# Ten pairs of a mixer's input projection by seven block products, the strided groups through scratch

## The chip, the cores and the metric

One core of a Trainium2 chip runs the whole kernel. The metric is the device time of one execution in microseconds; the time before is 2790.25 us, the median of three runs (2789.18 to 2790.53).

## The reference, cut to what matters

Two layers (`DEPTH = 2`) over 1024 tokens of 1024 features, all in float32. Each layer is a mixer and a gated feed-forward network:

```python
h = rmsnorm(x, norm1[l])
proj = h @ w_in[l]                       # 1024 x 5120
qa, ka, va, qb, kb, vb, gate_pre = jnp.split(proj, splits, axis=-1)
o_a = dilated_mixture(...qa, ka, va)     # 12 heads of 64: three groups of four, dilation 1, 4 and 16
o_b = stick_breaking_attention(...qb, kb, vb)   # 4 heads of 64
gates = jax.nn.sigmoid(gate_pre + b_gate[l])
merged = g_a * (o_a @ w_br[l, :OUT_A]) + g_b * (o_b @ w_br[l, OUT_A:])
x = x + merged @ w_o[l]
h2 = rmsnorm(x, norm2[l]); up = h2 @ w_up[l]     # conv, gelu, product, w_down
```

The 5120 columns of `w_in` are 40 chunks of 128: for mixer A six chunks each of q, k and v (two for each of its three groups), for mixer B two each of q, k and v, and 16 gate chunks. `dilated_mixture` weighs the three groups of a head slot by their softmax denominators.

## The kernel before

**Precision.** Each float32 operand of a large product is split into a rounded part and its remainder (`split`: a cast on ScalarE, L115, and a subtraction on VectorE, L116). A product of two split operands is three matmuls (hi x hi, lo x hi, hi x lo; `product`, L141 to L143). The normed input lies in `H[n]`, n being the half of the tokens (512 each), features on the partitions in eight blocks. One chunk of 128 output columns is 2 halves x 8 blocks x 3 = 48 matmuls of 128x512.

**Feed-forward network.** 20 of its 22 up-projections (`up`, a gate chunk and a value chunk together) are already worked out by seven block products in place of eight. The operands are cut in two by two blocks; sums of weight blocks are formed per pair on GpSimd and VectorE (L1139, L1140, L1144, L1149), sums of the input's blocks (`S[1]` to `S[4]`) once a layer; `seven` issues one block product of 4 x 3 = 12 matmuls, and three additions on VectorE put the seven results together. The down-projection is done so too.

**Mixer.** `head` works out v, k and q of mixer B's first pair of heads (four chunks). Then `attend` walks over 36 items: 16 stick-breaking ones (B), 4 near ones of group 0 (N), 16 far ones (T) that take the groups of dilation 4 and 16 together for one head slot and one residue r. An item is a list of small steps: scores, then alternately the turning of probabilities (transposes into bank `t`, split into p1h and p1l) and the application to the values (bank `o`). Between the steps `attend` calls `dense.advance(rate)`, which takes steps of six projection matmuls from a `Dense` object. Its `main` list holds the chunks that attention waits for (names like `b1`, `00`, `v1`), each with the items that must be done first; its `fill` list holds the 16 gate chunks, which nobody waits for. `RATE` gives the dense steps per attention step for the B, N and the two halves of the T items. The next item's scores are worked out among the steps of the item before, if its operands are there. TensorE's order is exactly the order of this walk (a manual schedule); the other engines' and SyncE's DMA queue's orders are set by a scheduler from the same program.

**Strided groups.** Groups 1 and 2 keep k and q in SBUF, each with its remainder, in an order by residue (`view`, `grid`: tokens r, r+4, ... next to each other); their values come out with features on the partitions and are transposed (`values_tiled`, bank v_t, L426) into an SBUF tile each. Everything stays in SBUF from projection to use.

**End of attention.** After the last far item of a pair of head slots, `join` (L743 on) reads the near group's statistics from scratch (sn), forms the weights by small operations (L755 to L764), writes them to scratch (df, L765), reads them back spread over partitions (fn, ft, L770), scales and adds (L771, L775, L776). `dense.finish()` then issues what is left of the dense work; then `on` and `ob` are split into the operands oh_a, ol_a, oh_b, ol_b, and 32 branch products (bank br_ps, weights br_w) follow, gated by gates read back from scratch (gin), then w_o.

Of the kernel before, what the change touches and what calls it, by code (L numbers as in the profile page):

```python
# [15 lines left out]
P = 128  # L16
# [16 lines left out]
PT = 5  # L33
# [7 lines left out]
RATE = (0.68, 0.85, 1.0, 0.8)  # L41
# [8 lines left out]
def trunk_kernel(ctx, tc, x, norm1, w_in, b_gate, w_br, w_o, norm2, w_up, conv_w, conv_b, w_down, norm_f, out, depth=None, probe=None):  # L50
# [50 lines left out]
    gd = dr.tile([NF // 2, 7, P, 2, HF], F32, name="gd")  # L101
    dn = [dr.tile([4, T], F32, name=f"dn{i}") for i in range(2)]
# [8 lines left out]
    def big(name, dtype=F32):  # L111
        return sb.tile([P, 2, T], dtype, tag="e8", bufs=6, name=name)

# [67 lines left out]
    class Dense:  # L181

        def __init__(self):
            self.main, self.fill, self.done = [], [], set()
            self.now = self.nxt = None
            self.due = 0.0

        def choose(self):  # L190
            if self.main and self.main[0][1] <= self.done:
                name, _, gen = self.main.pop(0)
            elif self.fill:
                name, gen = None, self.fill.pop(0)
            else:
                return None
            next(gen)
            return name, gen

        def step(self):  # L200
            while True:
                if self.now is None:
                    self.now = self.nxt or self.choose()
                    if self.now is None:
                        return False
                    self.nxt = self.choose()
                if next(self.now[1], 0) != 0:
                    return True
                self.done.add(self.now[0])
                self.now = None  # L210

        def advance(self, rate):
            self.due += rate
            while self.due >= 1.0:
                self.due -= 1.0
                if not self.step():
                    self.due = 0.0

        def until(self, names):
            while not set(names) <= self.done:  # L220
                assert self.step(), (names, self.done)

        def finish(self):
            while self.step():
                pass

# [77 lines left out]
    def new_x(n):  # L304
        X[n] = sb.tile([P, KD, HF], F32, tag=f"x{n}", name=f"x{n}")
# [4 lines left out]
    def norm_add(n, e, first=False, sub=slice(0, HF), adds=None):  # L310
# [6 lines left out]
        act.activation(sq, X[n][:, e, sub], AF.Square)  # L317
# [3 lines left out]
    def gain_in(n, e, sub=slice(0, HF)):  # L321

        x = X[n][:, e, sub]
# [36 lines left out]
    def norm(n, gain, tag, then=None, keep=False):  # L360
# [17 lines left out]
        for e in range(KD):  # L378
            hf = kept_f32(n, e) if keep else small("hf")
            dve.scalar_tensor_tensor(hf, X[n][:, e, :], gain[:, e : e + 1], rb, ALU.mult, ALU.mult)  # L380
# [9 lines left out]
    def values(key, l, off, tag):  # L390
        w = weights(w_in[l][:, off : off + 256], 256)
        yield
        vt = R[key] = sb.tile([P, 8, 4, P], F32R, tag=tag, name="v_" + tag)
        yield from values_part(vt, w, range(4))

    def values_part(vt, w, ms):
        for m in ms:
# [13 lines left out]
            vv = vt[:, 2 * m : 2 * m + 2, :, :]  # L411
# [4 lines left out]
    def values_tiled(key, l, off, tag):  # L416


        w = weights(w_in[l][:, off : off + 256], 256)
        yield  # L420
        vt = R[key] = sb.tile([P, 8, 4, P], F32R, tag=tag, name="v_" + tag)

        def turn(c, n, f):
            tp = bank("ps", "v_t")
            for r in range(4):
                pe.transpose(tp[:, r * P : (r + 1) * P], f[:, r * P : (r + 1) * P], ident)  # L426
            tv = tp.rearrange("p (r h c) -> p r h c", r=4, h=2)
            vv = vt[:, 4 * n : 4 * n + 4, 2 * c : 2 * c + 2, :]
            act.copy(vv[:, :, :, 0:64], tv)
            dve.tensor_tensor(vv[:, :, :, 64:128], tv, f32(vv[:, :, :, 0:64]), ALU.subtract)  # L430

        last = None
        for n in range(2):
            for c in range(2):
                o = bank("ps", "v_ps")
                yield from product(o, [((wh[:, c * P : (c + 1) * P], wl[:, c * P : (c + 1) * P]), h_part(n, k)) for k, (wh, wl) in enumerate(w)])
                f = small("vf")
                act.copy(f.rearrange("p (r j) -> p r j", r=4), grid(o, True))
                if last:
                    turn(*last)  # L440
                last = (c, n, f)
                yield
        yield
        turn(*last)
        yield


    def view(t, tiled, n):

        if tiled:  # L450
            return t.rearrange("p (r n j) -> p n r j", r=4, n=2)[:, n, :, :]
        return t[:, n * HF : (n + 1) * HF]

    def grid(o, tiled):
        return o.rearrange("p (j r) -> p r j", r=4) if tiled else o

    def keys_half(kt, w, n, tiled):
        o = bank("ps", "k_ps")
        yield from product(o, [(w[k], h_part(n, k)) for k in range(KD)])
        og = grid(o, tiled)  # L460
        ka, kb = view(kt[:, 0, :], tiled, n), view(kt[:, 1, :], tiled, n)
        act.copy(ka[0:64], og[0:64])
        act.copy(kb[64:128], og[64:128])
        dve.tensor_tensor(ka[64:128], og[0:64], f32(ka[0:64]), ALU.subtract)
        dve.tensor_tensor(kb[0:64], og[64:128], f32(kb[64:128]), ALU.subtract)
        yield

    def queries_half(q, w, n, tiled, scale):
# [3 lines left out]
        og = grid(o, tiled)  # L472
        qa, qb, la, lb = (view(a[:, i, :], tiled, n) for a in (qt, ql) for i in range(2))
        for q2, src in ((qa, og[0:64]), (qb, og[64:128])):
            act.mul(q2[0:64], src, scale)
            act.mul(q2[64:128], src, scale)
        dve.scalar_tensor_tensor(la[0:64], og[0:64], scale, f32(qa[0:64]), ALU.mult, ALU.subtract)
        dve.scalar_tensor_tensor(lb[64:128], og[64:128], scale, f32(qb[64:128]), ALU.mult, ALU.subtract)
# [10 lines left out]
    def keys(key, l, off, tiled):  # L489
# [3 lines left out]
        for n in range(2):  # L493
            yield from keys_half(kt, w, n, tiled)

    def queries(key, l, off, tiled, scale):
# [3 lines left out]
        for n in range(2):  # L500
            yield from queries_half(q, w, n, tiled, scale)

    def head(l):
# [9 lines left out]
        vt = R["vb"] = sb.tile([P, 8, 4, P], F32R, tag="x0", name="vb")  # L513
# [3 lines left out]
        for n in range(2):  # L517
            yield from keys_half(kt, wk, n, False)
            yield from queries_half(q, wq, n, False, SCALE)
# [3 lines left out]
    def scores(o, s, q, k, qs, ks):  # L523
        qt, ql = q
        pe.matmul(o, qt[:, s, qs], k[:, s, ks], start=True, stop=False, skip_group_check=True)
        pe.matmul(o, ql[:, s, qs], k[:, s, ks], start=False, stop=True, skip_group_check=True)  # L526
# [17 lines left out]
    def stick_item(pr, s, qp):  # L544
# [6 lines left out]
        def score(a):  # L551
# [6 lines left out]
            for c0 in range(0, L, 512):  # L558
                w = min(512, L - c0)
                z = bank("s", "z")  # L560
                scores(z[:, :w], s, q, k, slice(i * P, i * P + P), slice(c0, c0 + w))
# [20 lines left out]
        def apply(kb):  # L582
# [4 lines left out]
            for j in range(2):  # L587
                c = P if last and j else 0
                for p in (0, 1):
                    pe.matmul(  # L590
                        o[:, c:256],
                        vt[:, kb + j, hd, :],
# [5 lines left out]
            if last:  # L598
                fold(ob[64 * s : 64 * s + 64, pr, qp * 256 : (qp + 1) * 256], o)

# [4 lines left out]
    def near_item(pr, s):  # L605
        if s == 0:
            R["st0", pr] = sb.tile([P, 2, 2, 8], F32, tag="st0", bufs=2, name="st0")
        if "on" not in R:
            R["on"] = big("on")
# [4 lines left out]
        def score(m):  # L614
# [7 lines left out]
            for j in range(2):  # L622
# [3 lines left out]
                scores(zz, s, q, k, slice(b * P, b * P + P), slice((b - 1) * P + c, b * P + P))  # L626
# [17 lines left out]
        def apply(i, some, n, first, last):  # L644
# [4 lines left out]
            for kb, bs in some:  # L649
                c0, nb = (bs[0] - 4 * n) * P, len(bs) * P  # L650
                for p in (0, 1):
                    pe.matmul(
                        o[:, c0 : c0 + nb],
                        vt[:, kb, slot, :],
# [36 lines left out]
    def far_item(pr, s, r, share):  # L691
        slot = 2 * pr + s
        qk = [(R["q1", pr], R["k1", pr]), (R["q2", pr], R["k2", pr])]
# [834 lines left out]
```

## Time and profile before

| | |
|---|---|
| median of three runs | 2790.25 us |
| profiled execution: time, span | 2795.43 us, 2793.3 us |
| mean granted TensorE clock | 0.995 |
| TensorE busy, matmuls | 2723.8 us (98%), 13306 |
| VectorE, ScalarE, GpSimd busy | 67%, 47%, 19% |
| DMA | 355.5 MB, mean 127 GB/s |

The profile is of one execution. An engine's busy time is the sum of the stretches in which it had work; a group's mean is the duration of one instruction, and consecutive matmuls overlap, so their means add up to more than the busy time. The mixer of layer 0 takes about the first 650 us, that of layer 1 about 1400 to 2050 us. In the page's 40 slices TensorE is at nine tenths or more everywhere but the first, GpSimd is at zero or one tenth in the mixers, and the DMA engines are at one to three tenths there, with four to eight around the merges.

### The profile page before, as it was taken

Reading aid. Unit: us, or ns where it says so; the run is one execution under the profiler, and the core shown is the slowest. Engines: PE = TensorE matmul, PEld = TensorE weight load, DVE = VectorE, ACT = ScalarE, POOL = GpSimd, SP = SyncE. Lnnn points to the kernel's source line nnn. Section 1 sums busy time; section 2 is a strip of 40 time slices with the busy share of each in tenths; the row PEclk is TensorE's granted clock in tenths of the full one; section 3 lists DMA queues with packets and bytes.
Section 4 is the critical chain, followed back from the end, with each engine's and each line's share of the span. In section 5 each row is a group of like instructions: output and inputs, shape, how many; then the busy total and the mean of one; then the engine's idle time right before and its main releaser. Section 6 shows DMA issues by size and latency. Waiting matters only on the chain. (4 is left out here: it accounts for less than half of the span.)

```text
span 2793.3 us, 36113 instructions
## 1 busy us (share of the span) xinstructions
PE 2723.8 (98%) x13306; PEld 2278.0 (82%) x13306; DVE 1875.2 (67%) x2796; ACT 1326.2 (47%) x2410; POOL 518.1 (19%) x376
## 2 busy tenths in 40 slices
PE   8999999999999999999999999999999999999999
PEld 8878888888877778778888788888788787777888
DVE  5875434455778888897657754344658788888865
ACT  5655544454445545432345654335545455554225
POOL 0000000012134333331110000000212343443200
PEclk9999999999999999999999999999999999999999
DMA  3011113164334443688411111122822434436863
GB/s 122 24 46 54 36 53 80 61 212 132 87 113 160 142 151 129 217 317 300 154 50 35 42 43 46 58 72 71 262 88 78 151 130 149 164 138 240 336 230 121
DMA packets 285884, 355.52 MB, mean 127 GB/s; under 512 B 21532, under 2 KB 222604, under 8 KB 285196
## 3 DMA queue, kind: packets, MB, share of 16 engines
q1 hardware_dynamic: 285708, 353.22, 37.6%
q8 instruction: 105, 1.72, 0.2%
q14 instruction: 71, 0.58, 0.1%
HBM read 247.13 MB, written 106.04 MB: 126 GB/s over the span
## 5 line engine op out<-in xcount | busy, mean ns | idle before, releaser
L116 DVE TENSOR_TENSOR w_lo<-w_raw,w_hi 128x512 fp32r<-128x512 f32 x232 | 163.7, 709 | 147.6 <-ACT w_hi L115 139.0
L116 DVE TENSOR_TENSOR w_lo<-up_a,w_hi 128x512 fp32r<-128x512 f32 x240 | 231.7, 966 | 38.0 <-ACT w_hi L115 37.9
L115 ACT CAST w_hi<-w_raw 128x512 fp32r<-128x512 f32 x232 | 143.8, 621 | 201.0 <-PE o_ps L142 67.2
L115 ACT CAST w_hi<-up_a 128x512 fp32r<-128x512 f32 x240 | 149.4, 622 | 173.6 <-PE u_b L1124 38.5
L141 PE MATMUL g_ps<-hh,w_hi 128*128 128x512 f32 x512 | 211.6, 413 | 1.1 <-DVE v_x L430 1.1
L1284 DVE TENSOR_TENSOR x<-x,d_ps 128x512 f32<-128x512 f32 (+1 forms) x228 | 152.3, 671 | 82.7 <-PE d_ps L1278 81.8
L143 PE MATMUL g_ps<-hh,w_lo 128*128 128x512 f32 x512 | 201.1, 393 | 0.0
L142 PE MATMUL g_ps<-hl,w_hi 128*128 128x512 f32 x512 | 200.7, 392 | 0.0
L1003 POOL TENSOR_TENSOR cv<-cv 128x512 f32<-128x512 f32 x88 | 126.0, 1444 | 266.2 <-DVE g L116 130.1
L485 POOL MEMSET ql<- 64x1024 f32 x16 | 15.3, 955 | 831.4 <-PE z L526 643.2
L116 DVE TENSOR_TENSOR g<-cv,g 128x512 fp32r<-128x512 f32 x154 | 168.2, 1102 | 0.1
L1123 PE MATMUL u_a<-hh,w_hi 128*128 128x512 f32 x320 | 127.3, 398 | 19.4 <-ACT g L115 15.6
L1276 PE MATMUL d_ps<-gd_in,w_hi 128*128 128x512 f32 (+1 forms) x340 | 131.1, 385 | 5.8 <-ACT g L115 5.8
L1277 PE MATMUL d_ps<-gd_in,w_hi 128*128 128x512 f32 (+1 forms) x340 | 131.2, 386 | 0.0
L1278 PE MATMUL d_ps<-gd_in,w_lo 128*128 128x512 f32 (+1 forms) x340 | 131.0, 385 | 0.0
L1125 PE MATMUL u_a<-hh,w_lo 128*128 128x512 f32 x320 | 126.0, 394 | 4.1 <-DVE w_lo L116 4.1
L115 ACT CAST g<-cv 128x512 fp32r<-128x512 f32 x154 | 93.4, 620 | 75.4 <-DVE g L116 43.6
L1124 PE MATMUL u_a<-hl,w_hi 128*128 128x512 f32 x320 | 125.8, 393 | 0.0
L1123 PE MATMUL u_a<-t_hi,w_hi 128*128 128x512 f32 x320 | 124.6, 389 | 0.4 <-ACT u L1157 0.4
L1125 PE MATMUL u_a<-t_hi,w_lo 128*128 128x512 f32 x320 | 124.5, 389 | 0.0
L1124 PE MATMUL u_a<-t_lo,w_hi 128*128 128x512 f32 x320 | 124.5, 389 | 0.0
L143 PEld LDWEIGHTS g_ps<-hh,w_lo 128*128 128x128 f32 x512 | 96.1, 188 | 22.0
(335 smaller groups left out, 8056.5 us busy)
## 6 DMA issues: line engine op xcount, KB each, us to landing
gd<-g SPq DMA_DIRECT2D x154, 512.0 KB, 3.1
gd_in<-gd SPq DMA_DIRECT2D x154, 512.0 KB, 6.0
w_raw<-in_w_in_dram SPq DMA_DIRECT2D x160, 256.0 KB, 3.0
up_a<-in_w_up_dram SPq DMA_DIRECT2D x80, 512.0 KB, 4.5
wd_raw<-in_w_down_dram SPq DMA_DIRECT2D x22, 1024.0 KB, 9.1
gs<-gt SPq DMA_DIRECT2D x64, 256.0 KB, 2.1
gin<-gs SPq DMA_DIRECT2D x32, 512.0 KB, 4.4
w_raw<-in_w_o_dram SPq DMA_DIRECT2D x64, 256.0 KB, 2.8
```

Of the source, the lines that this page charges most:

```text
L115: act.copy(hi, src)
L116: dve.tensor_tensor(lo, src, f32(hi), ALU.subtract)
L141: pe.matmul(o, lh, rh, start=(first and i == 0), stop=False, skip_group_check=share)
L142: pe.matmul(o, lh, rl, start=False, stop=False, skip_group_check=share)
L143: pe.matmul(o, ll, rh, start=False, stop=(last and i == n - 1), skip_group_check=share)
L1123: pe.matmul(o, w[0][:, c], rh, start=(first and i == 0), stop=False, skip_group_check=True)
L1124: pe.matmul(o, w[0][:, c], rl, start=False, stop=False, skip_group_check=True)
L1125: pe.matmul(o, w[1][:, c], rh, start=False, stop=(last and i == 3), skip_group_check=True)
L1276: pe.matmul(o[:, sub], wh[:, c], gh[:, sub], start=(i == 0 and k in (0, 4, 5)), stop=False, skip_group_check=True)
L1277: pe.matmul(o[:, sub], wh[:, c], gl[:, sub], start=False, stop=False, skip_group_check=True)
L1278: pe.matmul(o[:, sub], wl[:, c], gh[:, sub], start=False, stop=(i == m - 1), skip_group_check=True)
L1284: dve.tensor_tensor(x, x, o[:, sub], ALU.add)
```

## The change

Of the 36 chunks that `attend` handles in a layer, 16 stay as they are: k and q of mixer B's second pair, values, k and q of group 0, and eight gate chunks (`PLAIN = 8`). The other 20 are worked out as ten pairs (`pair`): values, k and q of groups 1 and 2 (six pairs) and eight gate chunks (four pairs). A pair has seven block products of 12 matmuls, like `up`.

- `Dense` gets the lists `plain`, `seven` and `side`. The plain chunks come first; pairs start when the near items' scores are done (`N11s`) and no plain chunk is left. Six steps of a pair (`READY`) are prepared ahead: two loads, sums of weight blocks, splits.
- `block_sums` forms the sums `S[1]` to `S[4]` of the input's blocks a layer from H's parts, during the near items: 24 operations on GpSimd, 16 on VectorE and 16 splits.
- k and q of a strided group are written to scratch (`tk`), with q's remainder above a block of zeros that is filled once at the start (`none`); values go to `tv`. Each far item reads its own block (`fetch_kq`, 128x1536, and `fetch_v`, 128x512), two items' k and q and four items' values ahead; an item waits until `LEAD = 6` dense steps after its k and q were asked for.
- SBUF: x, the values, `on`, the fetched blocks and the sum share one tag `xa` of four tiles of 8 KB a partition. `ob` waits in scratch (`obd`) and is read back before the merge; x is moved in halves. `PT` is 6 for 5, the second half's rate 0.85 for 0.8.
- The gates' bias is added in the sigmoid, in two operations of 128x512 each, no longer when the gate is copied out.
- Two hooks, the split of `ob` and `on` and the first loads of the merge, are called from the last pair if attention is over by then, and otherwise after the dense work.

```diff
-PT = 5
+PT = 6
-RATE = (0.68, 0.85, 1.0, 0.8)
+RATE = (0.68, 0.85, 1.0, 0.85)
+PLAIN = 8
+LEAD = 6
...
+    def pair(dense, l, offs, tiled, put):
...
+        raw = sb.tile([P, 4, 512], F32, tag="ql", bufs=2, name="in_a")
+        for c in range(2):
+            nc.sync.dma_start(...w_in[l][:, offs[c] : offs[c] + P]...)
+        a11, a12, a21, a22 = (raw[:, i, :] for i in range(4))
+        yield
+        u = sb.tile([P, T], F32, tag="wr", bufs=NRAW, name="u")
+        u1, u2 = u[:, HF:T], u[:, 0:HF]
+        pool.tensor_tensor(u2, a11, a21, ALU.subtract)
+        pool.tensor_tensor(a21, a21, a22, ALU.add)
...
+        pa, pc = bank("ps", "i_a"), bank("ps", "i_c")
+        yield from seven(pa, w1, half(1, 0), True, True)
+        act.copy(view(u1), grid(pa))
+        w7 = piece(u2)
+        yield
+        yield from seven(pc, w5, S[1], True, True)
+        act.copy(view(u5), grid(pc))
+        w2 = piece(a12)
+        yield
+        yield from seven(pa, w6, S[2], False, True)
+        act.copy(view(u2), grid(pa))
+        w4 = piece(a22)
+        dense.last(0)
...
+        yield from seven(pc, w3, half(0, 1), False, True)
+        dve.tensor_tensor(view(u2), view(u2), grid(pc), ALU.add)
+        put(0, 0, u2, False)
...
+        yield from seven(pa, w7, S[3], False, True)
+        dve.tensor_tensor(view(u5), view(u5), grid(pa), ALU.add)
+        put(1, 0, u5, False)
+        dense.last(1)
...
+        pb = bank("ps", "i_b")
+        yield from seven(pb, w2, half(1, 1), True, True)
+        dve.tensor_tensor(view(u1), view(u1), grid(pb), ALU.add)
+        put(0, 1, u1, False)
...
+        for word in seven(pa, w4, S[4], False, True):
+            yield "turn"
+            yield
+        put(1, 1, grid(pa), True)
...
+    def fetch_kq(i):
+        t = R["kq", i] = sb.tile([P, 6, 256], F32R, tag="xa", bufs=4, name="t_kq")
+        nc.sync.dma_start(f32(t), tk[i // 8][i // 4 % 2, i % 4])
...
         dense.main = [
-            *kq("b", 1, set(), P, False, SCALE),
-            ("v0", set(), values("v0", l, OFF_VA, "x1")),
-            *kq("0", 0, {"B07s"}, 0, False, -SCALE),
-            *kq("0", 1, {"B17s"}, P, False, -SCALE),
-            ("v1", {"B17"}, values_tiled("v1", l, OFF_VA + 256, "x0")),
-            *kq("1", 0, {"N01s"}, 256, True, -SCALE),
-            *kq("2", 0, {"N11s"}, 512, True, -SCALE),
-            ("v2", {"N11"}, values_tiled("v2", l, OFF_VA + 512, "x1")),
-            *kq("1", 1, {"T07s"}, 256 + P, True, -SCALE),
-            *kq("2", 1, {"T07s"}, 512 + P, True, -SCALE),
+            *kq("b", 1, set(), P, SCALE),
+            ("v0", set(), values("v0", l, OFF_VA), False),
+            *kq("0", 0, {"B07s"}, 0, -SCALE),
+            *kq("0", 1, {"B17s"}, P, -SCALE),
+            (None, {"N11s"}, pair_v(dense, l, 1), True),
+            *((None, {"N11s"}, pair_kq(dense, l, g, 0), True) for g in (1, 2)),
+            (None, {"N11s"}, pair_v(dense, l, 2), True),
+            *((None, {"N11s"}, pair_kq(dense, l, g, 1), True) for g in (1, 2)),
         ]
...
         attend(dense, items)
-        dense.finish()
...
+        branches()
...
+        dense.hooks = [in_two, begin]
+        dense.finish()
+        for n in range(2):
+            new_x(n)
```

More of the change, by code (lines that the diff above doesn't have):

```diff
@@ L414, in values_part @@
             yield
[L416 to L445, printed above, removed]
@@ new lines, in pair_v, with turn, put @@
+    def pair_v(dense, l, g):
+        def turn(c, n, f):
+            tp = bank("s", "v_t")
+            for r in range(4):
+                pe.transpose(tp[:, r * P : (r + 1) * P], f[:, r * P : (r + 1) * P], ident)
+            tw = tp.rearrange("p (r h c) -> p r h c", r=4, h=2)
+            vv = sb.tile([P, 4, 2, P], F32R, tag="p4", bufs=4, name="vv")
+            act.copy(vv[:, :, :, 0:64], tw)
+            dve.tensor_tensor(vv[:, :, :, 64:128], tw, f32(vv[:, :, :, 0:64]), ALU.subtract)
+            for h in range(2):
+                there = tv[c][h, :, :, g - 1, n * P : (n + 1) * P]
+                nc.sync.dma_start(there.rearrange("r p c -> p r c"), f32(vv[:, :, h, :]))
+            if (c, n) == (1, 1):
+                dense.done.add(f"v{g}")
+        def put(c, n, x, psum):
+            f = x
+            if psum:
+                f = small("vf")
+                act.copy(f.rearrange("p (r j) -> p r j", r=4), x)
+            dense.at(2, lambda: turn(c, n, f))
+        off = OFF_VA + 256 * g
+        return pair(dense, l, (off, off + P), True, put)
@@ L779, in gate, with pair_gate, put @@
+    def pair_gate(dense, l, e):
+        def put(c, n, x, psum):
+            t = x
+            if psum:
+                t = small("gt")
+                act.copy(t, x)
+            nc.sync.dma_start(gs[e, n, :, c, :], t)
+        return pair(dense, l, (OFF_G + e * P, OFF_G + D + e * P), False, put)
     def gate(l, c):
```

383 lines of the change are left out of this document (272 added, 111 removed).

## The prediction

> **What bounds the kernel now.** I read the page first, its shares and TensorE's groups:
>
> ```profile
> span 2793.3 us, 36113 instructions
> PE 2723.8 (98%) x13306; PEld 2278.0 (82%) x13306; DVE 1875.2 (67%) x2796; ACT 1326.2 (47%) x2410; POOL 518.1 (19%) x376
> L143 PE MATMUL g_ps<-hh,w_lo 128*128 128x512 f32 x512 | 201.1, 393 | 0.0
> ```
>
> TensorE is busy 98% of the span and no other engine comes near. The 393 ns of a group are pipelined durations; what a matmul costs is its distance to the next. The timeline of TensorE inside a projection shows it:
>
> ```profile
> 467.06 0.39 PE L141 MATMUL k_ps<-hh,w_hi 128*128 128x512 f32 x1
> 467.29 0.39 PE L142 MATMUL k_ps<-hl,w_hi 128*128 128x512 f32 x1
> 467.52 0.39 PE L143 MATMUL k_ps<-hh,w_lo 128*128 128x512 f32 x1
> 467.74 0.39 PE L141 MATMUL k_ps<-hh,w_hi 128*128 128x512 f32 x1
> ```
>
> Three matmuls in 0.68 us: 0.2267 us each. The windows of the mixers say how full TensorE is where the change works (second column: TensorE's busy time in 70 us; the column behind POOL is its granted clock):
>
> ```profile
> 280.00:350.00 70.00, 67.73 (x346) 56.81 (x345) 32.79 (x76) 35.30 (x83) 1.90 (x2) 0.98 0.14 38
> 350.00:420.00 70.00, 68.02 (x347) 56.49 (x346) 22.87 (x48) 28.57 (x59) 0.00 (x0) 1.00 0.17 53
> 490.00:560.00 70.00, 70.00 (x382) 59.79 (x381) 30.27 (x70) 34.01 (x75) 0.00 (x0) 1.00 0.21 66
> 560.00:630.00 70.00, 70.00 (x339) 58.13 (x339) 37.93 (x61) 39.00 (x62) 9.07 (x7) 1.00 0.67 213
> ```
>
> The far attention (about 420 to 571) and the way into the merge have no hole at all; VectorE is at 43% there. So a matmul taken away is worth its 0.2267 us, as long as the rest still covers every wait. Which waits it covers now, the timeline at the end of layer 0's attention shows (ScalarE, VectorE, SyncE's queue):
>
> ```profile
> 558.45 0.08 DVE L719 DVE_READ_ACCUMULATOR2_ANT st<- 128x1 f32 x1
> 565.71 0.38 SPq L765 DMA_DIRECT2D df<-sf  x1
> 570.64 1.27 SPq L770 DMA_DIRECT2D ft<-df  x2
> 577.82 2.09 DVE L775 TENSOR_TENSOR ft<-ot,ft 128x512 f32<-128x512 f32 x2 [1.50 <-DMA ft<-df]
> 579.95 1.23 DVE L776 TENSOR_TENSOR on<-on,ft 128x1024 f32<-128x1024 f32 x1
> 581.21 1.14 ACT L115 CAST oh_a<-on 128x512 fp32r<-128x512 f32 x2 [4.17 <-DVE on L776]
> ```
>
> The last statistics are read at 558.5, `join` sends its factors to scratch (df) at 565.7 and gets them back spread (fn, ft); branch A's operand is ready 582 to 583. The last apply on TensorE starts at 570.8; then it works through 132 gate matmuls, until the branch products begin at 600.9. Those 30 us hide the whole round trip.
>
> **The change, part by part.** The sum is made against the profiled execution's 2795.4 us; the median, 2790.25, is 5.2 below it and gets the same difference.
>
> 1. *Products.* A pair costs 7x4x3 = 84 matmuls for 96; ten pairs in each of two layers save 240. All else on TensorE keeps its count in the built program (64 value transposes, 256 far score and 256 far apply matmuls). 240 x 0.2267 = **-54.4 us**.
>
> 2. *The end of attention.* This decides. In the changed program's order on TensorE the last dense matmul of a layer stands ahead of the last three transposes and eight applies of the far items before the last two; then come 16 score matmuls, 12 transposes and 16 applies of the last two items and at once the branch products: nothing dense is left. I time the bare chain from its start, by rows. Transpose to apply 1.74 us (566.91 to 568.65), eight applies 0.9: 2.65. Scores to last statistic of an item 1.8 (548.64 to 550.4), its follower 1.3 more, and a fold's 0.7 on VectorE ahead of both: 6.5. `join`'s small operations took 7.3 (558.5 to 565.7) among six of 0.7 us that are fewer now: I take 3.7, so df goes out at 10.2. From df to the first use of ft 12.1 (13.9 and 12.7 for the joins at 446.8 and 1947.4): 22.3. L775, L776 and the cast until the first branch matmul 4.0: 26.3. TensorE has 6 us of work in it (two scores of 0.92, five transpose groups of 0.33, six of 0.41). 20.3 us idle per layer: **+41**. Bounds 15 (df at 8, ft back in 9) to 28 (ft 5 later, see the second rival). [...]
>
> ```profile
> 300.00:305.00 5.00, 3.79 (x26) 3.22 (x24) 3.21 (x11) 3.02 (x8) 1.05 (x2) 1.00 0.39 110
> 305.00:310.00 5.00, 3.94 (x16) 3.16 (x16) 3.09 (x8) 3.18 (x9) 0.85 (x1) 0.68 0.18 52
> ```
>
> 2.3 us of holes, then a granted 0.68 over 5 us: 1.6 us lost. I put 1.8 per layer: **+3.6**. [...]
>
> 3. *Stalls that go.* The two windows above lose 2.27 and 1.98 us, layer 1 the same (2.31, 1.99): transposes of the strided values that wait for the copy just ahead (v_t on vf, 1.5 and 1.2), and banks behind them. With 1.6 of clock each time that is 11.8 us. Now a transpose stands 12 matmuls behind its product. I take **-9**.
>
> 4. *Stalls that come.* Each pair: 7 splits for 4, three adds, copies, on VectorE about 15 operations of 0.69 = 10 us beside 19 us of TensorE, so it isn't the bound. The pairs have the order of the up-projection's, whose stage loses 1.7 us in 70, to a bank read by the gating, which pairs lack. The scratch writes and reads (3 to 6 us to landing) lie a pair ahead, but on SyncE's queue t_v and t_kq, which wait for their buffer's last reader, stand ahead of the next pair's weights. The block sums (24 GpSimd operations of 1.3 to 1.4 us, 31 to 34 us) run beside some 80 us of near attention; ScalarE's casts of them can hold up its exps by a few us. No row shows either wait; between 0 and 25 us in all (next paragraph) I take 0.3 per pair: **+6**. [...]
>
> 5. *The start.* Four 512 KB zero fills of scratch stand in SyncE's order ahead of the second half of the first value weights, where the DMA share is 0.8 to 1.0 (2 to 14 us). 2 MB at the 300 GB/s of those windows is 7 us, half of it hidden by the norm chain: **+3.5** (0 to 7).
>
> Through scratch for ob, x in halves and the bias in the sigmoid (two of about 0.68 for one of 1.06, 13 us more ScalarE in the merges, where it is at half load): 0, since TensorE's 2.7 us per chunk covers them; about 2 us if it didn't.
>
> Sum: -54.4 + 41 + 3.6 - 9 + 6 + 3.5 = -9.3: 2786.1, or **2781** against the median.
>
> **Rivals.** *A wait per pair (slower).* Place: a pair's second product needs the bank that the last product of the pair before leaves only after ScalarE and VectorE have read it; cover is one product of 12 matmuls, 2.7 us. For: in the up-projection that kind of wait (u_a on ScalarE's g) costs 1.26 us at a time, 7 times in 280 us, and here exps and casts of far items stand in both queues. Against: two reads of 0.6 and 0.7 fit in 2.7. At 1.26 for each of 20 pairs, 25.2 for the 6 in the sum: +9.9, 2800. It decides from about 1.05 us per pair. *A longer round trip.* In layer 1's queue one 1 MB load of x stands ahead of df and one between df and fn; w_down's 1 MB loads took 9.1 us to land. If they push ft back by 7 us per layer, +14: 2795, no visible change or slower. *A shorter one (faster).* With nothing competing on VectorE, df goes out at 8 and ft is back in 9: 15 us idle per layer, -10.6, and without new stalls -6: 2764. *The change saves nothing* if the far stage follows VectorE: 43% now, some 70% after; I give that no chance of its own.
>
> **How the numbers follow.** A measurement of this kernel can tell about 0.2%, 5.6 us. Forecast 0.42 (faster 0.30, same 0.12, since 3 us in any term carry it across); shorter trip 0.18, faster; wait per pair 0.17, slower; longer trip 0.13 (same 0.06, slower 0.07); the start and the sums at their upper ends 0.10 (same 0.04, slower 0.06). Faster 0.48, same 0.22, slower 0.30. The range goes from the shorter trip, 2764, to the wait per pair with the start's 7 and two us per layer more in the chain, 2808; the likeliest case alone is 2775 to 2788.
>
> **What would show it.** TensorE should have 240 matmuls less and one hole of about 20 us in each layer, right ahead of br_ps, released by ScalarE's oh_a, with ft's landing behind it, and a clock below 1 after it; the v_t waits gone; stages with pairs at 97% or more. If that hole is below 12 us or above 28, step 2 is wrong; if TensorE idles over 1 us per pair ahead of i_c, step 4 is.

## The result and the profile after

The changed kernel takes 2820.5 us (median of 4 runs, 2815.6 to 2822.9) where the kernel before takes 2790.4 (4 runs, 2789.2 to 2793.0): a ratio of 1.0104, 95% interval 1.0087 to 1.0122. It is 30 us slower; the prediction was 2781, and its range ended at 2808. The profiled execution took 2819.5 us, 24.1 more than that of before, with a span of 2817.7 and a mean granted clock of 0.983 (0.995 before).

The page, span and first rows:

```profile
span 2817.7 us, 36591 instructions
PE 2692.9 (96%) x13066; PEld 2247.1 (80%) x13066; DVE 2001.3 (71%) x2968; ACT 1354.3 (48%) x2494; POOL 658.4 (23%) x469
```

The 240 matmuls are gone (13306 before) and TensorE is busy 31 us less, yet the span grew: TensorE waits. The windows that the prediction showed, now of the changed kernel (second column TensorE's busy time, the column behind POOL its clock):

```profile
280.00:350.00 70.00, 69.65 (x368) 58.66 (x368) 50.11 (x109) 41.19 (x98) 5.83 (x4) 0.98 0.27 80
350.00:420.00 70.00, 70.00 (x318) 57.67 (x317) 35.23 (x50) 29.40 (x52) 13.99 (x10) 1.00 0.57 153
490.00:560.00 70.00, 66.58 (x347) 56.26 (x347) 41.97 (x85) 30.51 (x68) 9.17 (x7) 0.95 0.62 189
560.00:630.00 70.00, 56.42 (x285) 45.80 (x284) 43.04 (x83) 39.46 (x80) 4.46 (x4) 0.88 0.59 189
```

The first two, with the pairs, are as full as predicted: no wait per pair, and the v_t waits are gone. The other two were at 70.00 before. The largest surprise lies in a window that the prediction did not show, the near attention of layer 0. First before, then the changed kernel:

```profile
210.00:280.00 70.00, 69.52 (x384) 59.10 (x382) 40.93 (x84) 40.21 (x92) 3.79 (x4) 1.00 0.17 53
```

```profile
210.00:280.00 70.00, 59.77 (x310) 49.94 (x309) 40.51 (x74) 35.63 (x84) 34.36 (x26) 0.92 0.17 57
```

TensorE loses 10 us and a twelfth of its clock, no engine but GpSimd does more, and GpSimd's 24 new operations are the block sums. ScalarE's timeline there shows what it waits for (start, duration, operation, in brackets the idle time before it and who ended it):

```profile
251.87 0.62 ACT L123 CAST t_hi<-h_sum 128x512 fp32r<-128x512 f32 x1 [6.09 <-POOL h_sum L873]
...
260.62 0.62 ACT L123 CAST t_hi<-h_sum 128x512 fp32r<-128x512 f32 x1 [5.88 <-POOL h_sum L873]
261.15 0.40 ACT L680 ACTIVATE p<-p,st 128x128 f32<-128x128 f32 x1
...
276.38 0.62 ACT L123 CAST t_hi<-h_sum 128x512 fp32r<-128x512 f32 x1 [5.59 <-POOL h_sum L873]
276.91 0.50 ACT L680 ACTIVATE p<-p,st 128x256 f32<-128x256 f32 x1
```

Three times ScalarE stands about 6 us at a cast of a block sum; with shorter ones its waits for h_sum add up to 20.1 us. Behind the second and the third the exps of the near items (L680) stand next in its queue: VectorE had read their statistics (st, L679) by 257.6 and 269.9 us, and they start at 261.15 and 276.91, behind the casts. The operand casts p0h (the rounded probabilities of the near items) come later still. TensorE waits for these (us in all, times, longest):

```profile
PE o L700 <- ACT p0h L123: 9.3, 2, 6.4
```

The first of the three stops doesn't reach TensorE, which is busy 5.00 us in each 5 us from 245 to 255. The second does, and a lower clock follows:

```profile
255.00:260.00 5.00, 1.22 (x6) 0.65 (x4) 2.58 (x6) 0.00 (x0) 5.00 (x4) 0.87 0.31 105
260.00:265.00 5.00, 2.21 (x6) 1.76 (x7) 3.40 (x7) 2.87 (x9) 5.00 (x4) 0.50 0.00 0
```

A ledger by TensorE's landmarks puts the 24.4 us of span in three places. The landmarks are pt_c (the transposes of small constants just ahead of attention), the first st_t (the statistics of the first two of the four near items) and the last branch product. Between pt_c and st_t both kernels have 1200 matmuls in layer 0; the 120 matmuls saved per layer lie between the last two landmarks.

| stretch | before, layers 0 / 1 | after | difference |
|---|---|---|---|
| start to pt_c of layer 0 | 65.8 | 73.6 | +7.8 |
| pt_c to st_t (stick attention, half of the near) | 213.7 / 212.7 | 227.9 / 228.4 | +14.2 / +15.7 |
| st_t to the last branch product | 371.9 / 368.4 | 363.7 / 365.2 | -8.2 / -3.2 |
| all else | | | -1.9 |

In the third row 27.2 us of products per layer are saved, so 19 and 24 us are lost again in it. Its hole is the predicted one (SyncE's queue, VectorE, ScalarE, then TensorE's wait, layer 0):

```profile
598.46 0.37 SPq L828 DMA_DIRECT2D df<-sf  x1
609.35 1.98 DVE L838 TENSOR_TENSOR ft<-ot,ft 128x512 f32<-128x512 f32 x2 [1.30 <-DMA ft<-df]
612.63 1.14 ACT L123 CAST oh_a<-on 128x512 fp32r<-128x512 f32 x2 [1.55 <-DVE on L839]
```

```profile
PE br_ps L149 <- ACT oh_a L123: 8.5, 1, 8.5
PE z L571 <- DVE st L780: 4.3, 3, 2.1
```

The last dense matmul ended at 588.2: df went out 10.3 us later (10.2 forecast), ft was first used after 21.2 (22.3), the branch products went on after 25.1 (26.3). Of the second line 0.9 us belong to this hole; the other 3.4 are another loss, at 533 to 538 among the far items: VectorE is busy with join's wide operations of the first pair of heads (529 to 537) while the scores of the next item wait in their banks.

### The profile page after: what moved, and what is told of

Its sections match the earlier page's. It is cut to its first block, busy times and chain, and to the rows that moved or that the text cites. A ratio compares the mean times of both kernels' runs of the same rounds, so it can differ in the third digit from the quotient of the medians.

```text
span 2817.7 us, 36591 instructions
## 1 busy us (share of the span) xinstructions
PE 2692.9 (96%) x13066; PEld 2247.1 (80%) x13066; DVE 2001.3 (71%) x2968; ACT 1354.3 (48%) x2494; POOL 658.4 (23%) x469
## 5 line engine op out<-in xcount | busy, mean ns | idle before, releaser
L124 DVE TENSOR_TENSOR w_lo<-w_raw,w_hi 128x512 fp32r<-128x512 f32 x152 | 113.6, 753 | 67.2 <-ACT w_hi L123 63.5
L123 ACT CAST w_hi<-w_raw 128x512 fp32r<-128x512 f32 x152 | 93.9, 620 | 120.1 <-PE o_ps L150 66.5
L123 ACT CAST w_hi<-in_a 128x512 fp32r<-128x512 f32 x120 | 74.5, 620 | 146.9 <-PE i_a L855 61.0
L124 DVE TENSOR_TENSOR w_lo<-in_a,w_hi 128x512 fp32r<-128x512 f32 x120 | 87.8, 732 | 80.3 <-ACT w_hi L123 80.1
L614 DVE TENSOR_TENSOR_SCAN stay<-stay,zero 128x128 f32<-128x128 f32 (+3 forms) x64 | 86.9, 1357 | 38.7 <-ACT stay L612 38.5
L1526 PE MATMUL d_ps<-gd_in,wd 128*128 128x512 f32 (+1 forms) x292 | 114.0, 390 | 0.0
L1528 PE MATMUL d_ps<-gd_in,wd 128*128 128x512 f32 (+1 forms) x292 | 112.9, 387 | 0.0
```

The source lines that it names most:

```text
L123: act.copy(hi, src)
L124: dve.tensor_tensor(lo, src, f32(hi), ALU.subtract)
L614: dve.tensor_tensor_scan(rev, rev, zero[:, 0:1].to_broadcast([P, L]), 1.0, ALU.mult, ALU.add)
L1526: pe.matmul(o[:, sub], wh[:, c], gh[:, sub], start=(i == 0 and k in (0, 4, 5)), stop=False, skip_group_check=True)
L1528: pe.matmul(o[:, sub], wl[:, c], gh[:, sub], start=False, stop=(i == m - 1), skip_group_check=True)
```

## Experiments

A number of us "returned" is the ratio of the changed kernel, 1.0104, less that of the run, times 2790; two such ratios together are good to about 6 us.

### The block sums: moved, made on VectorE, left out

*Casts three sums later* (the split of a sum is emitted three sums behind):

```
-            split(*S[t][i], r)
+            casts.append(lambda: split(*S[t][i], r))
...
+            if p >= 3: casts.pop(0)()
```

> The changed kernel with one thing moved: ScalarE's cast and VectorE's remainder of each block sum (split after the three GpSimd operations in block_sums.first) are put in their queues three block sums later; the 24 GpSimd operations stay where they are. Theory A (queue order): the near attention of each layer loses some 14 to 16 us because ScalarE's casts stand ahead of its exps and wait for GpSimd, 4 us per block sum. Then most of it returns: 11 to 14 us per layer, 22 to 28 in all, 2793 to 2799. Rival B (contention): VectorE and GpSimd hold each other up while the sums run, whatever stands in which queue. Then less than 5 us in all return: above 2815. A's row: the waits of ScalarE on GpSimd's h_sum (6.1, 5.9, 5.6 us in layer 0) are gone, and the window 210 to 280 us has TensorE above 67 us busy instead of 59.8.

Ratio 1.0060 (1.0045 to 1.0075): 12 us returned, between the two theories. The waits on h_sum became fewer, not none: the second four sums still come out of GpSimd after their casts stand in the queue (5.8 us at 275.5). Undecided.

*The three operations of a sum on VectorE* (`pool.tensor_tensor` becomes `dve.tensor_tensor`, three lines):

> The changed kernel with the three operations of each of the eight block sums on VectorE instead of GpSimd: 24 VectorE operations of about 0.69 us, 16.6 us per layer, in a stage where VectorE is busy about 57 of 70 us. Theory A (ScalarE's queue waits for slow GpSimd): a sum takes 2 us instead of 4 and no separate engine is waited for, so 8 to 14 us per layer return: 2792 to 2804. Rival B (VectorE is the short engine there): VectorE fills up and the near stage stays as long or gets longer: 2815 to 2830.

Ratio 1.0000 (0.9991 to 1.0010): 29 us returned, twice 14 to 15 of them between pt_c and st_t (213.0 and 213.5). The same window of this kernel:

```profile
210.00:280.00 70.00, 69.03 (x379) 58.50 (x378) 60.01 (x117) 45.46 (x104) 1.90 (x2) 1.00 0.25 80
```

VectorE rises from 40.5 to 60.0 us and TensorE is full: VectorE was not the short engine (the 57 of 70 us above are not those of this window). A sum's three operations of 0.69 us now take half of GpSimd's time, and ScalarE's waits for them shrink from 20.1 to 1.9 us.

*No sums* (S[1] to S[4] are plain blocks, no operation is issued):

> The changed kernel without the block sums: the three sum operands are replaced by plain blocks of the normed input, so the pairs' products multiply other data and nothing is added, cast or subtracted for the sums. It gives what the sums cost in all. Theory A and rival B both expect 28 to 34 us less than the changed kernel (14 to 16 per layer in the near stage and a little in VectorE's queue): 2787 to 2793. If less than 15 us return, the loss between the first attention product and the end of the near items is not the sums'.

Ratio 0.9993 (0.9983 to 1.0002): 31 us returned, the whole price of the sums. Of it they still cost about 2 on VectorE, which is within the error.

### The zero fills later

The memset and the four DMAs stand behind the first drive() instead of ahead of setup.

> The changed kernel with the four 512 KB zero fills of scratch put into SyncE's queue after the first projections of layer 0 instead of ahead of the value weights. Theory (the start's +7.8 us ahead of the first attention item is the fills'): the first pt_c comes at 66 to 68 us instead of 73.6, 5 to 8 us return, 2812 to 2816. Rival (the start is late for another reason, such as the new copies in the norm chain): pt_c stays at 72 or later and the time within 2 us of 2820.

Ratio 1.0075 (1.0060 to 1.0091): 8 us returned, and pt_c comes at 65.6 us as before the change (65.8). From there to st_t it takes 229.6 us for 227.9, as in the other runs that leave the sums as they are (227.9 to 229.8), so no loss shows where the fills stand now. The theory holds.

### Cover for the end of attention

*Two plain gate chunks kept back until the last far item:*

```
-        dense.plain = [gate(l, c) for c in range(PLAIN)]
+        dense.plain = [gate(l, c) for c in range(PLAIN - 2)]
+        dense.tail = [[None, gate(l, c), False, 0] for c in range(PLAIN - 2, PLAIN)]
```

They read half(0, 0) after the fourth block sum has been written over it, so their values are of other data; their work is the same.

> The changed kernel with two of the eight plain gate chunks (96 matmuls, 21.8 us) kept back until the last far item: their weights are fetched and split when all pairs are done, their products stand on TensorE behind the last apply and ahead of the branch products. Theory (step 2 of the prediction: nothing dense is left to cover the round trip through join): the hole ahead of br_ps and the low clock behind it go, 16 to 20 us per layer, so 2781 to 2789 against the changed kernel's 2820.5. Rival (the near items starve instead, since they have 96 matmuls less beside them): half or more is given back between the first attention product and the end of the near items, 2800 to 2820.

Ratio 1.0068 (1.0053 to 1.0083): 10 us returned, not 32 to 40.

```profile
490.00:560.00 70.00, 64.81 (x337) 54.44 (x336) 39.14 (x81) 31.03 (x68) 8.93 (x6) 0.95 0.54 166
560.00:600.00 40.00, 34.45 (x180) 28.71 (x180) 23.11 (x53) 21.07 (x45) 0.00 (x0) 0.91 0.57 179
600.00:670.00 70.00, 70.00 (x340) 57.94 (x339) 46.05 (x64) 47.95 (x82) 21.40 (x16) 1.00 0.65 221
```

The hole ahead of br_ps is gone (the last line), but the far stage lost more in front of it. The rival named the wrong place: pt_c to st_t took 229.8 us for 227.9, with as many matmuls in it. Behind st_t the pairs moved up beside the last near items (first product of a pair at 326.2 us for 351.7); so the far items had 96 matmuls less, and they ran out earlier (last product of a pair at 576.1 us for 588.0).

*The round trip without its return* (join ends behind df for the second pair of heads):

```
+        if pr:
+            return
         fn = sb.tile([P, T], F32, tag="p4", bufs=4, name="fn")
```

> The changed kernel without the last part of join for the second pair of heads: its factors still go to scratch, but are not fetched back, and the four VectorE multiplications and additions that use them are left out (branch A's operand for that pair is the near attention's alone). It prices the bare round trip. Theory (step 2): without fn and ft the branch products start 16 us earlier per layer (12.1 us from df to ft, 4 us of VectorE and cast) and the clock stays higher: 32 to 42 us less, 2779 to 2789. Rival (the hole is set by other operands of the branch, br_w or the gates): less than 10 us in all, above 2810.

Ratio 1.0043 (1.0028 to 1.0058): 17 us returned, half of what was expected. The branch products went on at 602.2 instead of 613.3, but at 0.80 us a matmul, for 0.39 elsewhere, behind a new last operand:

```profile
599.08 0.38 PE L796 MATMUL o<-p1l,t_v 128*128 128x256 f32 x1 [0.71 <-DVE p1l L124]
602.22 0.80 PE L149 MATMUL br_ps<-oh_a,br_w 128*128 128x512 f32 x1 [2.58 <-ACT br_w L123]
604.11 0.80 PE L151 MATMUL br_ps<-oh_a,br_w 128*128 128x512 f32 x1 [0.67 <-DVE br_w L124]
```

What is left is the bare chain of the last two items and the branch weights' casts behind it on ScalarE.

*The kernel before without its leftover* (its fourth RATE 0.8 becomes 1.35, so 6 of 132 gate matmuls are left):

> The kernel before with one number changed: the rate at which gate matmuls are used beside the last eight far items is 1.35 instead of 0.8, so that 6 instead of 132 gate matmuls are left ahead of the branch products. Nothing is removed; it prices the round trip through join without cover. Theory (step 2): from the last statistics (558.5 us) to branch A's operand (583) are 24.5 us, some 12 of which the transposes, applies and gate matmuls of the last item still fill: 12 to 16 us idle per layer and about 2 of clock, so 28 to 36 us more than before, 2818 to 2826, a ratio of 1.010 to 1.013. Rival (cover is only moved: what stands earlier saves stalls there): under 10 us more, since the far stage has none to save, this needs the hole to be short.

Ratio 1.0052 (1.0037 to 1.0068): 14.5 us more, between the theory and its rival.

```profile
600.00:620.00 20.00, 13.65 (x54) 10.48 (x53) 11.98 (x17) 12.07 (x16) 2.59 (x2) 0.74 0.58 201
```

The round trip without a leftover does open a hole, 6.35 us and 5 of clock in layer 0. The matmuls used earlier stand between the last statistics (580.0) and the last apply (599): of the some 28 us from the statistics to the end of oh_a's casts all but 6.3 stay covered. So a hole is the chain's length less whatever work stands anywhere behind its start, not only behind its last apply.

*Pairs spread thinner over the far items:*

```
-RATE = (0.68, 0.85, 1.0, 0.85)
+RATE = (0.68, 0.85, 1.0, 0.6)
-LEAD = 6
+LEAD = 3
```

> The changed kernel with two numbers changed: a far item is released 3 instead of 6 dense steps after its fetch, and the pairs are used beside the last eight far items at a rate of 0.6 instead of 0.85. Then 90 matmuls of the last pair stand behind the last apply. Theory (cover is short by the matmuls saved, wherever it stands): the hole ahead of br_ps goes, part of it comes back as waits of scores and applies among the far items, 10 to 25 us less than the changed kernel: ratio to the kernel before 1.002 to 1.007. Rival 1 (the far items need no more cover than the 36 matmuls each that this leaves them): all of the hole returns, 35 to 43 us less, ratio 0.995 to 0.998. Rival 2 (three steps are too few for the fetch to land, t_kq late at every item): no gain or slower, 1.010 or more.

Ratio 0.9917 (0.9901 to 0.9933): 52 us returned, more than either theory or rival had. With it alone the changed kernel is faster than the one before.

```profile
490.00:560.00 70.00, 70.00 (x411) 61.03 (x410) 46.54 (x104) 37.54 (x88) 9.02 (x7) 1.00 0.74 236
560.00:630.00 70.00, 67.14 (x330) 55.26 (x329) 52.61 (x84) 48.10 (x87) 13.14 (x11) 1.00 0.69 231
```

Both windows are repaired, the one at the end and the one at 490 to 560, with the same number of dense matmuls in the layer. Cover was not short in all: it was spent where the far items did not need it (which of the two numbers does how much of this was not tried). From st_t to the last branch product it now takes 340.2 and 339.1 us, 31.7 and 29.3 less than before the change.

### The saved product

Every pair's first block product twice (a line repeated in `pair`), in the changed kernel and later in the best one:

> The changed kernel with the first block product of every pair worked out twice (eight block products of 12 matmuls instead of seven, as many matmuls as the kernel before; the second overwrites the first). It prices the saved product alone. Theory (step 1): 240 matmuls at 0.2267 us, +54.4 us: 2870 to 2877. Rival (in the stages with pairs something other than TensorE sets the pace, so a product more falls partly into idle time): +35 us or less, below 2856.

> The best kernel so far (ratio 0.979) with the first block product of every pair worked out twice, as was done to the changed kernel, where the 240 matmuls cost 39 us. Theory (there 15 us of the product were paid for by waits among the far items that it covered; with the pairs spread better there are none): the full 54.4 us, ratio 0.998 to 1.000. Rival (a matmul in these stages is worth less than its 0.2267 us): about 39 us again, ratio 0.992 to 0.994.

In the changed kernel +39.6 us (1.0246; 1.0231 to 1.0261), between theory and rival: the added product also filled waits among the far items (window 490 to 560 back at 69.42 us and clock 1.00). In the best kernel (below, under "Together"), whose window of 490 to 560 is full, it costs 51 us (0.9977 against 0.9793): 54.4 within the error. Step 1's 0.2267 us per matmul stands.

### The mechanism of the sums

*GpSimd's work kept, ScalarE's casts cut loose:*

```
-            split(*S[t][i], r)
+            split(*S[t][i], f32(ah))
```

> The changed kernel in which the casts of the first eight block sums read the normed input's own block instead of GpSimd's result: the 24 GpSimd operations, the casts and the remainders all stay, in number and place, but no cast waits for GpSimd any more (the two sums in question are left out of the pairs' products). Theory A (ScalarE's queue: casts that wait for GpSimd stand ahead of the exps): all but 1 to 3 us of what leaving the sums out brought returns, 26 to 31 us, ratio to the kernel before 0.999 to 1.001. Rival B (GpSimd beside VectorE and ScalarE slows their operations): the contention is the same as in the changed kernel, so under 6 us return, ratio 1.008 to 1.010. Moving the casts three sums later returned 13 of about 31 us, between the two, and left waits of 12 us on GpSimd.

Ratio 1.0129 (1.0114 to 1.0144): slower than the changed kernel, so both theories failed as stated. The wait had moved to VectorE, which makes the other sums from GpSimd's:

```profile
269.78 9.65 DVE L883 TENSOR_TENSOR h_sum<-hh,h_sum 128x512 f32<-128x512 f32 x2 [14.39 <-POOL h_sum L873]
279.36 0.41 DVE L679 CUSTOM_DVE_ANT_0 p<-z,bias 128x256 f32<-128x256 f32 x1
```

14.4 us of waiting, and then two operations of which the trace's row for the tile gives the durations (shortest, median, longest in ns):

```profile
L883 DVE TENSOR_TENSOR h_sum<-hh,h_sum x2: 679/4866/9052, 269.8 to 278.8; 128x512 f32<-128x512 f32 x2
```

The second took 0.68 us, as such operations do elsewhere; the first took 9.05 and ended at 278.8, 0.5 us behind GpSimd's last (278.3). The near items' scores (L679) stand behind both.

*No reader left:* as above, and VectorE's further sums on tiles of their own:

```
-            r, (ah, al) = keep["r"][:, i, :], a()[i]
-            dve.tensor_tensor(r, f32(ah), r, ALU.subtract)
+            r, (ah, al) = small("h2"), a()[i]
+            dve.tensor_tensor(r, f32(ah), f32(al), ALU.subtract)
```

> The changed kernel with GpSimd's 24 operations kept, but without a reader: the casts read the normed input's own blocks, and VectorE's two operations for each of the other sums work on tiles of their own instead of GpSimd's result (the block sums are so left out of the pairs' products). In the run before this one the casts had been cut loose, but VectorE's operations still waited for GpSimd, 14.4 us in layer 0, and one of them, 0.69 us elsewhere, took some 9 us beside GpSimd. Theory A (waits in the queues): with no reader left, 26 to 31 us return, ratio 0.999 to 1.001. Rival B (contention: operations of VectorE beside GpSimd are stretched): less than 15 us return, ratio 1.005 to 1.009, and rows of VectorE between 245 and 280 us are above 1 us where the kernel before has 0.69.

Ratio 1.0017 (1.0000 to 1.0033): 24 us returned, a little under theory A's 26 and far from B's 15; its span, 2789.9 us, is that of the kernel without sums, 2790.0.

```profile
210.00:280.00 70.00, 68.92 (x380) 58.53 (x379) 53.00 (x96) 45.05 (x105) 36.22 (x26) 1.00 0.26 83
```

```profile
245.78 1.74 DVE L124 TENSOR_TENSOR w_lo<-w_raw,w_hi 128x512 fp32r<-128x512 f32 x1 [1.00 <-ACT w_hi L123]
...
263.37 1.77 DVE L124 TENSOR_TENSOR t_lo<-hh,t_hi 128x512 fp32r<-128x512 f32 x1
```

GpSimd is as busy as in the changed kernel (36.2 against 34.4 us) and some of VectorE's rows are stretched from 0.69 to as much as 1.77 us beside it, as B says; TensorE does not feel it (68.92 us busy, 69.52 in the kernel before). So 24 of the sums' 31 us, by this run, are waits in the queues for a chain of 24 GpSimd operations of 1.3 to 1.6 us, such as ScalarE's 6.09, 5.88 and 5.59 us above, with other work standing behind them. The other 7 (this run's ratio against that without sums) are about the error; whether stretched operations have a part in them is open.

### Together

*Sums on VectorE, fills later, two gate chunks kept back* (which read other data, as in e5_tail):

> The changed kernel with three edits together: the block sums' operations on VectorE (28.7 us less than the changed kernel measured against the kernel before), the zero fills after the first projections (7 us) and two plain gate chunks kept back for the end of attention (by step 2, 32 to 40 us). If the three are independent: 65 to 76 us less, 2745 to 2756, a ratio of 0.984 to 0.988 to the kernel before. Rival (with VectorE full beside the near items, 96 matmuls less of cover there cost what the tail gains): 2770 or more.

Ratio 0.9927 (0.9911 to 0.9944): 49 us returned, 37 of them the sums and the fills; the tail brought about as little as alone. The rival's outcome (2772 us), for the reason of e5_tail and not by VectorE's load: pt_c to st_t was 214.5 us.

*Sums on VectorE, fills later, LEAD 3 and rate 0.6;* and the same with the third RATE at 0.8:

> The block sums on VectorE, the zero fills after the first projections, and the release after 3 steps with the rate 0.6, in one kernel. If the three add up: 28.7 + 7 + the 10 to 25 of the release less than the changed kernel, 2760 to 2775, ratio 0.989 to 0.995. If all of the hole returns, 2742 to 2750, ratio 0.983 to 0.986.

> As the one before, with the rate beside the first eight far items at 0.8 instead of 1.0, so that 138 matmuls stand behind the last apply. The hole ahead of br_ps measured 17 to 24 us per layer, and 90 matmuls are 20.4 us: if these are enough, 48 more bring nothing, within 3 us of the one before, or lose some 5 us by less cover among the first items; if the hole is longer than 20 us, up to 8 us less.

Ratios 0.9793 (0.9776 to 0.9809), 2736 us, and 0.9831 (0.9813 to 0.9848). The first is the version that beats both kernels: 87 us under the changed one, 57 under the one before. It leaves nothing out. The 48 matmuls more at the end cost 10 us, more than expected.

*The sums back on GpSimd, paced; the pairs' GpSimd operations on VectorE:*

> The best kernel so far (sums on VectorE, fills later, release after 3 steps at a rate of 0.6; ratio 0.979) with the block sums back on GpSimd, but one sum at every second step and its cast three half-steps behind. Theory A: where the casts wait, what counts is that GpSimd needs 4 us per sum; paced at two steps per sum (about 5 us) few casts wait, and VectorE is spared 16 us per layer: within 4 us of the kernel with the sums on VectorE, 0.978 to 0.981. If the later sums run into the end of the near items, where they are needed at once: 5 to 15 us more, 0.981 to 0.985.

> The best kernel so far (ratio 0.979) with the three GpSimd operations ahead of each pair (two differences, one sum of weight blocks) on VectorE: 3 more operations of 0.69 us for VectorE per pair of about 19 us of TensorE. If VectorE beside GpSimd is stretched enough to matter among the far items: 2 to 6 us less. If GpSimd's part is harmless there: within 2 us, or up to 4 us more by VectorE's load, 0.979 to 0.981.

0.9818 (0.9803 to 0.9833) and 0.9789 (0.9772 to 0.9805). Pacing alone brings pt_c to st_t to 218.4 us, with all 24 GpSimd operations still beside the near items: about 10 of the 14 us of a layer are a question of what stands in front of what. The pairs' own GpSimd operations are harmless (0.9793 with them, 0.9789 without).

## Why the prediction was wrong

| step | forecast | shown by the runs |
|---|---|---|
| 1 and 3, products and v_t | -63.4 | -61.0 (31.7 and 29.3 in the third stretch, once the cover is back) |
| 2, end of attention | +44.6 | 52 returned, some 14 of it at 490 to 560 and its twin in layer 1 (3.4 and 3.3 us idle, and 0.05 of the clock over 70 us, in each), which step 2 did not have |
| 4, new stalls, of it the block sums | +6, "a few us" | the sums 31; no wait per pair |
| 5, start | +3.5 | 8 |
| sum | -9.3 | -61 + 52 + 31 + 8 = +30; measured +30.1 |

The first two rows come from one run, f1_lead: their sum, -9, repeats the third row of the ledger (-11.4), and only the split is new. The 31 and the 8 are measured by themselves.

*The step that failed is step 4.* It had the place (the near attention), the operations (24 at 1.3 to 1.4 us) and the mechanism ("ScalarE's casts of them can hold up its exps"), and mis-sized it: it set 31 to 34 us of GpSimd against 80 us of near attention, as if the chain could lie anywhere in those. The 24 operations run back to back from 245 to 278, and casts that need them stand in ScalarE's queue all along that stretch; two of its three long stops there became stops of exps, operand casts and TensorE, and the granted clock fell to 0.50. Even the stated upper end, 25 us for all new stalls, lay below the sums' 31 alone. Of the 39 us between the sum and the measurement step 4 holds 25, step 2 seven, step 5 four and a half, steps 1 and 3 two. With step 4 alone put right the sum would have come to 2806, just inside the range; the others carry it out.

*Step 2 was right* in mechanism and, in sum, nearly in size: the chain took what was forecast. Inside it the split was off. TensorE stood idle for 13.6 us of the 25.1 (layer 1: 16.2 of 27.2), not 20.3, the wait for oh_a being 8.5 (11.2) of it; and its work there, three branch products included, took 11.5 us (11.0), not 6, at a granted clock of 0.74 (0.73). That these two errors nearly make up for each other is luck. What it read about the clock from one stretch (300 to 310 us of the kernel before: holes, then a granted 0.68) came again: in the empty 5 us from 605 the granted clock was 0.50, and 0.79 still at 615 to 620, after TensorE had started again:

```profile
605.00:610.00 5.00, 0.00 (x0) 0.00 (x0) 1.87 (x2) 0.00 (x0) 0.00 (x0) 0.50 0.93 263
610.00:615.00 5.00, 1.70 (x3) 1.12 (x4) 3.85 (x5) 3.09 (x6) 0.00 (x0) 0.50 1.06 341
615.00:620.00 5.00, 5.00 (x21) 4.01 (x20) 3.04 (x5) 4.70 (x9) 0.00 (x0) 0.79 0.09 34
```

The 1.8 us per layer that it put on this were the author's estimate from that stretch, and no run shows the term by itself; what was measured is the granted clock of 0.74 (0.73) above. Nor is every hole followed by a lower clock: in the kernel before, after 2.40 us of idle TensorE ahead of 183.97 us it was 0.76 (185 to 190 us), after 2.42 us ahead of 1567.45 us it was 1.00 (1570 to 1575 us).

*Steps 1 and 3 were right*, with one thing missing: a product taken away is also cover taken away. In the changed kernel it was worth 40 us, not 54, since the far items then waited (3.4 us for the scores in layer 0, 3.3 in layer 1, and 3.5 of clock in each), waits that the product had covered.

*Step 5* reached its upper end and 1 us more: nothing of the 2 MB hides behind the norm, since the first value weights stand behind it and TensorE waited 4.7 us for their cast.

The rivals: the wait per pair did not come (no wait for a pair's bank stands among TensorE's waits of 300 to 600 and 1700 to 1960 us; it was the likeliest slower case, at 0.17). Some rows of VectorE are longer beside GpSimd: those of 128x512 took 0.67 to 1.77 us in g5_nobody_waits (245 to 280 us) and 0.68 to 0.69 in e2_sums_vec, where GpSimd is idle in that stretch. One row of 9.05 us (last section) is longer than any one GpSimd instruction beside it (1.25 us). In the changed kernel the stretching is off the path, or nearly so: GpSimd's work without a reader left TensorE nearly as full as in the kernel before (68.9 against 69.5 us in the window of 210 to 280).

## What to carry to other kernels

Work on a slow engine is not free because that engine is idle (here GpSimd: 1.3 to 1.6 us for a sum's operation that takes 0.69 on VectorE, and moving 24 of them a layer there returned 29 us): look at which queue reads its result, what stands behind that read, and put the producer that many microseconds ahead, or on an engine whose rows are shorter. When matmuls are taken out of a full TensorE, recount what they covered, at each place where a chain ends, and share out what is left again: here two numbers of the schedule were worth 52 us, as much as the saved products. A range for an unknown wait must reach at least to the whole length of the chain that is waited for.

## What was not expected of the hardware

- One VectorE operation of 0.68 us beside a run of GpSimd operations took 9.05 us in layer 0 of g1_cast_other, until just after GpSimd's last, while others beside GpSimd took 0.67 to 1.77 (g5_nobody_waits, 245 to 280 us). What decides between these was not tried.
- GpSimd's rows differ too: its operation on two 128x512 blocks took 1.25 us while VectorE waited or stood in that one row (g1_cast_other, 256 to 278 us), and up to 1.75 us among VectorE's own work (g3_best_paced, 255 to 266 us).
